# Spreading per-token factors over partitions: a trip through DRAM in place of transposes and selector products

## The chip, the cores and the metric

One core of a Trainium2 chip runs the whole program once. The metric is the device time of that execution in microseconds (us). TensorE multiplies matrices into PSUM, VectorE, ScalarE and GpSimd do the elementwise work, and transfers are issued from the queues of SyncE (SP), ScalarE and GpSimd. In the profile's rows PE is TensorE's matmuls, PEld its weight loads, DVE is VectorE, ACT ScalarE, POOL GpSimd; a name with a q behind it is that engine's own instruction queue.

## The reference, cut to what matters

The layer is a decoder block on 512 tokens of 1024 channels in float32. It has three mixers (gated delta rule, convolution, attention to a memory), merged through gates, and then a gated MLP. The change touches the gated delta rule alone, and there the keys k, four heads of 128 channels:

```
kb = k * beta[..., None]
A = jnp.where(strict, jnp.einsum('bnhid,bnhjd->bnhij', kb, k) * decay, 0.0)
T = lax.linalg.triangular_solve(eye + A, ...)      # inverse of eye + A
u = T @ (v * beta);  w = T @ (kb * exp(g));  then a scan over the chunks
```

Here k is L2-normed per token and head, so the factor of one token and head is beta over the norm of k. The kernel keeps k transposed (channels on partitions, tokens along the row), so a factor per token has to lie along the row, and the same row has to be on all 128 partitions.

## The kernel before, in words

**Tiling.** Activations are held as 128 channels x 512 tokens (S = 512). Every float32 operand of a projection is split into a rounded part and the rest (`split`, L147 to L154: a cast by ScalarE at L150, a subtraction by VectorE at L151), and each 128x128 tile of weights gives three matmuls (L271 to L273). I call those three matmuls a step; eight steps make one output tile of 128 channels, and eight weight tiles make one transfer of 512 KB, a chunk (`fetch`, L232; the transfer is L243).

**Order of the work.** The instructions of TensorE and of the SP queue run in the order of the source. Those of the other engines are ordered by the framework's planner, which simulates the program; a dependency without a semaphore (`paced`, L276, and `behind`, L107) tells only the planner that one instruction comes after another. The source order is made of generators: `run(main, (g, n))` (L158) takes one step of the projection `main`, then lets the background generator g go on by one turn for every n steps. `pause(n)` uses up n turns. The dictionary WAIT (L21) holds the pauses.

**The loops around the change.** The projections of k, q, v and z take 32 steps each (L943 to L951), then comes the first branch loop of 96 steps (L983). In the background run, one behind the other: `l2` (norms of k, transposed copies), `gdn_k` (L688), `base_load`, `gdn_q`, `base_inverse`, `invert` (L780), `scan` and `out`.

- `gdn_k` makes three factors per token and head on VectorE (L690 to L692), tokens on partitions, 128x16. The factor kbc is turned into rows by `rows` (L305): two VectorE instructions split it, four TensorE transposes put it on 8 partitions (L313), ScalarE copies it to krow (L314). A product with a selector column then spreads one head's row over 128 partitions (L703), and VectorE multiplies k with it from PSUM (L705). The products k times kb follow (L715), four blocks of eight 128x128 products, and VectorE multiplies in the decay (L716). Each block goes to DRAM (d_in, L717).
- `base_load` reads the diagonal 32x32 blocks back (L746), `base_inverse` inverts them on VectorE, 62 instructions in one dependent chain (L759, L762, in the rows also L118), stores the result to DRAM (L768, L769) and loads it back as tc32 (L772), all on the SP queue.
- `invert` puts the inverses of larger blocks together. It copies the blocks of tc32 into tm and tts (L794 on ScalarE, L797 on GpSimd, L799 on ScalarE), makes 64 products of 32x32 (L804), copies them out of PSUM to m1 (L807), and after six turns uses m1 in 128 products of 32x32 (L813, L814). Two more levels follow (L829, L838).

The weights are fetched three to four chunks ahead of the step that uses them, on the same SP queue.

Of the kernel before, what the change touches and what calls it, by code (L numbers as in the profile page):

```python
# [9 lines left out]
F32 = mybir.dt.float32  # L10
F32R = mybir.dt.float32r
AF = mybir.ActivationFunctionType
ALU = mybir.AluOpType
AX = mybir.AxisListType

P = 128
S = 512
# [1 line left out]
LAG = (5, 6, 2)  # L19

WAIT = {"mem": 4, "x": 30, "decay": 15, "scores": 1, "level": 6, "scan": 3, "out": 8,  # L21
        "k": 20, "head": 7, "krow": 6, "inverse": 16, "store": 5, "load": 14, "z": 4, "kk": 1, "ln": 30, "mix": 0}
WARM = 10

EARLY = 8
# [7 lines left out]
H = 4  # L33
NT = S // P
# [25 lines left out]
def hybrid_kernel(ctx: ExitStack, tc: tile.TileContext, xT, memT, xtok, mtok, wall, wdn, nfin, vecs, cms, y):  # L60
    nc = tc.nc
# [6 lines left out]
    dp = ctx.enter_context(tc.tile_pool(name="dp", bufs=1, space=bass.MemoryType.DRAM))  # L68
# [7 lines left out]
    def nm(p):  # L76
        uid[0] += 1
        return f"{p}{uid[0]}"
# [5 lines left out]
    def T(shape=(P, S), dt=F32, n="t"):  # L84
        i = slots.popleft()
        t = tp.tile(list(shape), dt, name=nm(n), tag=f"slot{i}")
        owner[t.tensor.name] = i
        return t

    def free(*ts):  # L90
        for t in ts:
            slots.append(owner.pop(t.tensor.name))

    def C(shape, dt=F32, n="c"):
        return cp.tile(list(shape), dt, name=nm(n))
# [4 lines left out]
    def G(shape=(P, S)):  # L100
        return psg.tile(list(shape), F32, name=nm("g"), tag="g")

    def SM(shape):
        return pss.tile(list(shape), F32, name=nm("sm"), tag="sm")

    A, G_, PE = nc.scalar, nc.gpsimd, nc.tensor
# [17 lines left out]
    V = _Vector()  # L124
# [5 lines left out]
    def f(t):  # L130
        return t.bitcast(F32)

    def sl(t):
        return slice(t * P, (t + 1) * P)
# [50 lines left out]
    def pause(n):  # L185
        for _ in range(n):
            yield
# [25 lines left out]
    ps = G()  # L213
# [62 lines left out]
    def paced(ins):  # L276

        tc.add_manual_dep(ins.ins, last[0].ins.name,
                          mybir.DependencyInfo(mybir.DependencyClass.NoSync, mybir.DependencyReason.DATA),
                          reason="pace")  # L280
# [24 lines left out]
    def rows(src, nt, nq, rt):  # L305

        hl = C((P, nt, 2 * nq), F32R)
        V.tensor_copy(hl[:, :, :nq], src)
        V.tensor_tensor(hl[:, :, nq:], src, f(hl[:, :, :nq]), op=ALU.subtract)
        yield from pause(1)  # L310
        ps = SM((P, S))
        for t in range(nt):
            PE.transpose(ps[:2 * nq, sl(t)], f(hl[:, t]), ident)  # L313
        A.copy(rt, ps[:2 * nq, :nt * P])  # L314
        yield

    def squares(tiles, add, pool=()):
# [118 lines left out]
    def C16():  # L436
        return C((P, NT, H))
# [5 lines left out]
    sel4 = const.tile([8, 4], F32R, name="sel4")  # L443
# [14 lines left out]
    def decay():  # L458
# [34 lines left out]
        V.tensor_copy(mg, ps[:, 3])  # L493
        yield from pause(3)
        yield from rows(mg, NT, H, grow)
        yield from pause(2)
        for h in range(H):
# [155 lines left out]
    q, k_, v = [], [], []  # L653
    qe, rk = C16(), C16()
    kbc, kgc, kdc = C16(), C16(), C16()
    at = [T((P, H, P), n="at") for _ in range(NT)]
# [6 lines left out]
    def cb(c16, t):  # L663
        return c16[:, t].unsqueeze(2).to_broadcast([P, H, P])
# [23 lines left out]
    def gdn_k():  # L688
        yield from pause(2)
        V.tensor_tensor(kbc, beta, rk, op=ALU.mult)  # L690
        V.scalar_tensor_tensor(kgc, kbc, -1.0, eg, op0=ALU.mult, op1=ALU.mult)
        V.tensor_tensor(kdc, ekd, rk, op=ALU.mult)  # L692
        yield from pause(WAIT["krow"])
        krow = T((8, S), F32R, n="krow")
        for h in range(H):
            kt = ktok[h][:, :NT - 1]
            G_.tensor_tensor(kt, kt, kdc[:, :NT - 1, h].unsqueeze(2).to_broadcast([P, NT - 1, P]), op=ALU.mult)
        yield from rows(kbc, NT, H, krow)
        yield from pause(2)
        kb = []  # L700
        for h in range(H):
            ps = G()
            PE.matmul(ps, sel4[:, h:h + 1].to_broadcast([8, P]), krow, start=True, stop=True)  # L703
            t = T(n="kb")
            V.tensor_tensor(t, k_[h], ps, op=ALU.mult)  # L705
            kb.append(t)
            yield
        free(krow)
        yield from pause(WAIT["kk"])
        wr = d_in.rearrange("(t b) x -> t (b x)", t=NT * H)[:, :P * P].rearrange("t (p i) -> p t i", p=P)  # L710
        for t in range(NT):
            G_.tensor_tensor(dec[t], dec[t], cb(rk, t), op=ALU.mult)
            ps = G((P, H, P))
            for h in range(H):
                PE.matmul(ps[:, h], k_[h][:, sl(t)], kb[h][:, sl(t)], start=True, stop=True)  # L715
            V.tensor_tensor(at[t], ps, dec[t], op=ALU.mult)  # L716
            A.dma_start(wr[:, t * H:(t + 1) * H], at[t])  # L717
            yield
        free(*kb)

    def gdn_q():
        yield from l2(qe, q, None)
# [57 lines left out]
    def invert():  # L780


        lo = [slice(64 * p, 64 * p + 32) for p in range(2)]
        up = [slice(64 * p + 32, 64 * p + 64) for p in range(2)]
        tc_ = tc32.rearrange("p (t h) a c -> p t h a c", t=NT)
        tm = [T((P, 2, H, 64), n="tm") for _ in range(2)]
        for t in range(NT):
            tts[t] = T((P, H, P), n="tt")
        for m in (*tm, *tts):
            G_.memset(m, 0.0)  # L790
        for b in range(NB):
            r = slice(32 * b, 32 * b + 32)
            for i in range(2):
                A.copy(tm[i][r, :, :, 32 * (b % 2):32 * (b % 2) + 32], tc_[r, 2 * i:2 * i + 2, :, 0])  # L794
            for t in range(NT):
                if t < 2:
                    G_.tensor_copy(tts[t][r, :, r], tc_[r, t, :, 1])  # L797
                else:
                    A.copy(tts[t][r, :, r], tc_[r, t, :, 1])  # L799
        ps = G((P, NT, H, 32))  # L800
        for t in range(NT):
            for h in range(H):
                for a, b in zip(lo, up):
                    PE.matmul(ps[b, t, h], at[t][a, h, b], tc_[a, t, h, 0], start=True, stop=True)  # L804
        m1 = T((P, NT, H, 32), n="m1")
        for b in up:
            A.copy(m1[b], ps[b])  # L807
        yield from pause(WAIT["level"])
        px, py = G((P, NT, H, 32)), G((P, NT, H, 32))
        for t in range(NT):  # L810
            for h in range(H):
                for a, b in zip(lo, up):
                    PE.matmul(px[b, t, h], tc_[b, t, h, 1], m1[b, t, h], start=True, stop=True)  # L813
                    PE.matmul(py[a, t, h], m1[b, t, h], tc_[b, t, h, 1], start=True, stop=True)  # L814
        for i in range(2):
            for b in up:
                V.tensor_scalar(tm[i][b, :, :, :32], px[b, 2 * i:2 * i + 2], -1.0, None, op0=ALU.mult)
        for t in range(NT):
            for a, b in zip(lo, up):
                A.activation(tts[t][a, :, b], py[a, t], AF.Copy, scale=-1.0)  # L820
        free(m1)
        yield from pause(WAIT["level"])
        a, b = slice(0, 64), slice(64, P)
        m1 = []
        for i in range(2):
            ps = G((P, 2, H, 64))
            for t in range(2):
                for h in range(H):
                    PE.matmul(ps[b, t, h], at[2 * i + t][a, h, b], tm[i][a, t, h], start=True, stop=True)  # L829
            m1.append(T((P, 2, H, 64), n="m1"))  # L830
            A.copy(m1[i][b], ps[b])
        free(*at, *tm)
        yield from pause(WAIT["level"])
        for i in range(2):
            ps = G((P, 2, H, 64))
            for t in range(2):
                for h in range(H):
                    PE.matmul(ps[a, t, h], m1[i][b, t, h], tts[2 * i + t][b, h, b], start=True, stop=True)  # L838
            for t in range(2):
                V.tensor_scalar(tts[2 * i + t][a, :, b], ps[a, t], -1.0, None, op0=ALU.mult)  # L840
        free(*m1)
        yield from pause(WAIT["level"])
# [70 lines left out]
    def out(t):  # L913
# [19 lines left out]
        if t == NT - 1:  # L933
            for z in sz:
# [8 lines left out]
    run(proj_conv(k_, 4), (gl, 1), (gd, 1), (gm, 2), (gc, 2))  # L943
    drain(gd)
    gk = chain(gl, gdn_k())
    run(proj_conv(q, 0), (gk, 1.3), (gm, 2), (gc, 3))
    drain(gm)
# [3 lines left out]
    run(proj_z(), (gp, 2))  # L951
    behind[0] = None
    gi = chain(gp, pause(WAIT["load"]), invert(), scan(0),
               rr(scan(1), out(0)), rr(scan(2), out(1)), rr(scan(3), out(2)), out(3))

# [75 lines left out]
    for o in range(KD):  # L1031
        a, b = T(dt=F32R, n="mgh"), T(dt=F32R, n="mgl")
# [359 lines left out]
```

## Time and profile before

| what | value |
|---|---|
| median of 3 runs | 848.01 us (847.92 to 849.87) |
| the profiled execution | 850.48 us, of which the traced span is 848.7 us |
| mean granted TensorE clock | 0.995 |
| TensorE matmul busy | 837.2 us, 99% of the span |
| VectorE, ScalarE, GpSimd busy | 71%, 46%, 10% |
| transfers | 123.22 MB, mean 145 GB/s |

A matmul's busy time is modelled and matmuls overlap, so how fast TensorE goes is read from the starts of its matmuls and not from its busy share. A row of the timeline has the start, the duration, the engine, the source line, the operation, what it writes and reads, its size and count, and in brackets the idle time before it with what ended it. A granted clock of 1.00 is 2.4 GHz, 0.50 is 1.2 GHz.

### The profile page before, as it was taken

How to read it: one execution, taken by the hardware profiler on the slowest of the kernel's cores; microseconds unless marked ns; L12 is line 12 of the kernel's file. 1: busy time of each engine (PE TensorE's matmuls, PEld its weight loads, DVE VectorE, ACT ScalarE, POOL GpSimd, SP SyncE). 2: the span in 40 equal slices, each digit the busy share in tenths (PEclk: the TensorE clock that was granted, in tenths of full speed). 3: DMA queues.
4: the chain of work that ended last, by engine and by line, in shares of the span. 5: the costliest groups of instructions: out<-in, count | busy, mean ns of one | idle time of the engine just before them, and what ended most of it. 6: DMA issues, size and time to landing. Idle time of an engine off the chain costs nothing.

```text
span 848.7 us, 11144 instructions
## 1 busy us (share of the span) xinstructions
PE 837.2 (99%) x4140; PEld 695.1 (82%) x4140; DVE 606.3 (71%) x954; ACT 388.0 (46%) x669; POOL 87.6 (10%) x101
## 2 busy tenths in 40 slices
PE   9999999999999999999999999999999999999996
PEld 7888788788887888888888888888888888888885
DVE  5885799859988999683266556666666656769863
ACT  7854675534235345452334344333333333657443
POOL 0100002500020001032000031111120110000001
PEclk9999999999999999999999999999999999999998
DMA  9753212242063122322244469696896882275662
GB/s 320 294 183 125 75 51 75 78 121 100 25 166 108 51 75 75 100 74 100 100 149 149 149 163 234 182 209 169 211 222 161 229 206 99 76 222 174 223 186 99
DMA packets 60949, 123.22 MB, mean 145 GB/s; under 512 B 18048, under 2 KB 20352, under 8 KB 60544
## 3 DMA queue, kind: packets, MB, share of 16 engines
q1 hardware_dynamic: 47424, 107.84, 38.0%
q0 software_dynamic: 6336, 11.54, 9.0%
q10 hardware_dynamic: 7136, 3.15, 1.3%
q8 instruction: 32, 0.52, 0.3%
q14 instruction: 21, 0.17, 0.1%
HBM read 118.83 MB, written 26.74 MB: 172 GB/s over the span
## 4 chain that ended last, share of the span: by engine, by line
PE 94%; DVE 4%; issue 1%; ACT 1%; POOL 0%; POOLq 0%; DVEq 0%; ACTq 0%
PE mm L271 19%; PE mm L272 18%; PE mm L273 18%; PE g L272 5%; PE g L273 5%; PE g L271 5%; PE g L1261 2%; PE g L1262 2%; PE g L1263 2%; PE mm L1262 2%; PE mm L1261 2%; PE mm L1263 2%; DVE wlo L151 1%; PE g L570 1%; PE g L572 1%
## 5 line engine op out<-in xcount | busy, mean ns | idle before, releaser
L150 ACT CAST whi<-raw 128x1024 fp32r<-128x1024 f32 (+1 forms) x167 | 171.6, 1028 | 277.1 <-PE mm L272 167.9
L151 DVE TENSOR_TENSOR wlo<-raw,whi 128x1024 fp32r<-128x1024 f32 (+1 forms) x167 | 201.3, 1205 | 77.5 <-ACT whi L150 76.6
L271 PE MATMUL mm<-hh,whi 128*128 128x512 f32 x352 | 142.6, 405 | 0.0
L273 PE MATMUL mm<-hh,wlo 128*128 128x512 f32 x352 | 137.6, 391 | 0.0
L272 PE MATMUL mm<-hl,whi 128*128 128x512 f32 x352 | 137.4, 390 | 0.0
L608 DVE SCALAR_TENSOR_TENSOR cc<-u,vec,cc 128x507 f32<-128x507 f32 (+19 forms) x120 | 86.7, 732 | 1.0
L273 PEld LDWEIGHTS mm<-hh,wlo 128*128 128x128 f32 x352 | 66.1, 188 | 14.3
L271 PEld LDWEIGHTS mm<-hh,whi 128*128 128x128 f32 x352 | 66.3, 188 | 13.1 <-issue 1.5
L272 PEld LDWEIGHTS mm<-hl,whi 128*128 128x128 f32 x352 | 66.4, 189 | 11.5
L271 PE MATMUL g<-fh,whi 128*128 128x512 f32 x176 | 69.1, 392 | 0.0
L271 PE MATMUL mm<-fh,whi 128*128 128x512 f32 x176 | 68.9, 392 | 0.0
L273 PE MATMUL mm<-fh,wlo 128*128 128x512 f32 x176 | 68.6, 390 | 0.0
L273 PE MATMUL g<-fh,wlo 128*128 128x512 f32 x176 | 68.6, 390 | 0.0
L272 PE MATMUL g<-fl,whi 128*128 128x512 f32 x176 | 68.6, 390 | 0.0
L272 PE MATMUL mm<-fl,whi 128*128 128x512 f32 x176 | 68.6, 390 | 0.0
L1096 POOL DMA_DIRECT2D q<-wdn x44 | 36.3, 1000 | 160.1 <-DMA q<-q 97.2
L1163 DVE TENSOR_TENSOR fg<-mm,rfb 128x512 f32<-128x512 f32 x22 | 15.2, 691 | 52.1 <-PE mm L273 52.1
L273 PEld LDWEIGHTS mm<-fh,wlo 128*128 128x128 f32 x176 | 33.1, 188 | 6.9
L273 PEld LDWEIGHTS g<-fh,wlo 128*128 128x128 f32 x176 | 33.0, 188 | 6.9
L272 PEld LDWEIGHTS mm<-fl,whi 128*128 128x128 f32 x176 | 33.1, 188 | 6.7
L271 PEld LDWEIGHTS mm<-fh,whi 128*128 128x128 f32 x176 | 33.0, 188 | 6.8
L271 PEld LDWEIGHTS g<-fh,whi 128*128 128x128 f32 x176 | 33.1, 188 | 6.7
(311 smaller groups left out, 1586.4 us busy)
## 6 DMA issues: line engine op xcount, KB each, us to landing
raw<-wall SPq DMA_DIRECT2D x120, 512.0 KB, 3.4
q<-wdn POOLq DMA_DIRECT2D x44, 256.0 KB, 6.4
raw<-q SPq DMA_DIRECT2D x44, 256.0 KB, 2.9
raw<-wdn SPq DMA_DIRECT2D x33, 256.0 KB, 3.4
q<-wdn SPq DMA_DIRECT2D x22, 256.0 KB, 4.5
q<-q SPq DMA_DIRECT2D x22, 256.0 KB, 4.9
x<-xT SPq DMA_DIRECT2D x16, 256.0 KB, 3.9
raw<-wall SPq DMA_DIRECT2D x8, 256.0 KB, 5.5
```

The costliest lines, as they stand in the source:

```text
L150: A.copy(hi, src)
L151: eng.tensor_tensor(lo, src, f(hi), op=ALU.subtract)
L271: PE.matmul(ps, hi, xh[k], start=(k == 0), stop=False)
L272: PE.matmul(ps, hi, xl[k], start=False, stop=False)
L273: last[0] = PE.matmul(ps, lo, xh[k], start=False, stop=(k == n - 1))
L570: PE.matmul(ps[h], hi, xh[k], start=(k == 0), stop=False)
L608: paced(V.scalar_tensor_tensor(a[:, s:], u[c][:, :S - s], vc("dww", c * 31 + 30 - s), a[:, s:], op0=ALU.mult, op1=ALU.add))
L1096: paced(G_.dma_start(dst[p - 3], b[p - 3], accum_op=ALU.add))
L1163: V.tensor_tensor(g, ps, rfb, op=ALU.mult)
L1261: PE.matmul(ps[m], h[:, o:o + P], hi, start=(p == 0), stop=False)
L1262: PE.matmul(ps[m], h[:, o:o + P], lo, start=False, stop=False)
L1263: last[0] = PE.matmul(ps[m], l[:, o:o + P], hi, start=False, stop=(p == NP - 1))
```

## The change

`rows` and the selector product stay for another factor (in `decay`); in `gdn_k` they are replaced. A new helper writes kbc to DRAM, turned round, by one transfer from SP, and after a pause reads each head's row back to all 128 partitions, by four transfers from SP. VectorE multiplies k with these rows in place. Pauses are changed: krow 6 to 3, the new krows 6, kk 1 to 6 and one more behind it, inverse 16 to 18. The four factor multiplications on GpSimd (L697) come three turns sooner. In `invert`, the block copies are put behind the 64 products and the copies to m1 in the source.

```diff
     def spread(dst, src, n, lag):
+        d = dp.tile([NT * n, P], F32, name=nm("rows"))
+        nc.sync.dma_start(d.rearrange("q p -> p q"), src.rearrange("p t h -> p (t h)"))
+        d = d.rearrange("(t h) p -> h t p", h=n)
+        yield from pause(lag)
+        for h in range(n):
+            dst.append(T((P, NT, P), n="row"))
+            nc.sync.dma_start(dst[h], d[h].unsqueeze(0).to_broadcast([P, NT, P]))
+        yield
...
-        krow = T((8, S), F32R, n="krow")
...
-        yield from rows(kbc, NT, H, krow)
-        yield from pause(2)
-        kb = []
+        row, kb = [], []
+        yield from spread(row, kbc, H, WAIT["krows"])
+        yield from pause(WAIT["kk"])
         for h in range(H):
-            ps = G()
-            PE.matmul(ps, sel4[:, h:h + 1].to_broadcast([8, P]), krow, start=True, stop=True)
-            t = T(n="kb")
-            V.tensor_tensor(t, k_[h], ps, op=ALU.mult)
+            t = row[h].rearrange("p t c -> p (t c)")
+            paced(V.tensor_tensor(t, k_[h], t, op=ALU.mult))
             kb.append(t)
-            yield
-        free(krow)
-        yield from pause(WAIT["kk"])
+            if h % 2:
+                yield
+        yield from pause(1)
...
         for m in (*tm, *tts):
             G_.memset(m, 0.0)
+        ps = G((P, NT, H, 32))
+        for t in range(NT):
+            for h in range(H):
+                for a, b in zip(lo, up):
+                    PE.matmul(ps[b, t, h], at[t][a, h, b], tc_[a, t, h, 0], start=True, stop=True)
+        m1 = T((P, NT, H, 32), n="m1")
+        for b in up:
+            A.copy(m1[b], ps[b])
         for b in range(NB):
...
-        ps = G((P, NT, H, 32))
-        for t in range(NT):
-            for h in range(H):
-                for a, b in zip(lo, up):
-                    PE.matmul(ps[b, t, h], at[t][a, h, b], tc_[a, t, h, 0], start=True, stop=True)
-        m1 = T((P, NT, H, 32), n="m1")
-        for b in up:
-            A.copy(m1[b], ps[b])
         yield from pause(WAIT["level"])
```

## Rows read from the trace of the kernel before

**Rows 1.** The page: busy time by engine, and the chain that ended last.
```profile
PE 837.2 (99%) x4140; PEld 695.1 (82%) x4140; DVE 606.3 (71%) x954; ACT 388.0 (46%) x669; POOL 87.6 (10%) x101
...
PE 94%; DVE 4%; issue 1%; ACT 1%; POOL 0%; POOLq 0%; DVEq 0%; ACTq 0%
```

**Rows 2.** Timeline of TensorE around the transposes L313 (start, duration, work).
```profile
162.74 0.39 PE L273 MATMUL mm<-hh,wlo 128*128 128x512 f32 x1
164.04 0.60 PE L313 MATMUL sm<-cm,c 128*8 128x128 f32 x4 [0.92 <-DVE c L309]
164.40 0.48 PE L271 MATMUL mm<-hh,whi 128*128 128x512 f32 x1
```

**Rows 3.** Timeline of TensorE from the first selector product L703 to L715.
```profile
167.01 0.39 PE L273 MATMUL mm<-hh,wlo 128*128 128x512 f32 x1
167.33 0.49 PE L703 MATMUL g<-krow,sel 8*128 8x512 f32 x1
...
168.09 0.39 PE L272 MATMUL mm<-hl,whi 128*128 128x512 f32 x1
...
171.28 0.49 PE L703 MATMUL g<-krow,sel 8*128 8x512 f32 x1
...
173.20 1.05 PE L715 MATMUL g<-kb,qkv 128*128 128x128 f32 x8
```

**Rows 4.** Timeline of TensorE around the products L813 and L814.
```profile
256.67 0.39 PE L272 MATMUL mm<-hl,whi 128*128 128x512 f32 x1
256.90 0.39 PE L273 MATMUL mm<-hh,wlo 128*128 128x512 f32 x1
258.15 0.21 PE L813 MATMUL g<-m,c 32*32 32x32 f32 x1 [0.86 <-ACT m L807]
...
259.93 0.56 PE L271 MATMUL mm<-och,whi 128*128 128x512 f32 x1
...
263.68 0.39 PE L271 MATMUL mm<-och,whi 128*128 128x512 f32 x1
```

**Rows 5.** Timeline of ScalarE from the first block copy to m1.
```profile
251.00 0.71 ACT L794 COPY tm<-c 32x256 f32<-32x256 f32 x2 [1.68 <-DMA c<-d_out]
...
257.52 1.18 ACT L807 COPY m<-g 32x512 f32<-32x512 f32 x2
```

**Rows 6.** Busy time by window: length, engines with counts, PEclk, DMA share, GB/s.
```profile
252.00:254.00 2.00, 2.00 (x25) 1.64 (x19) 2.00 (x4) 1.98 (x8) 1.92 (x5) 1.00 1.04 420
...
261.00:262.00 1.00, 1.00 (x4) 0.71 (x3) 1.00 (x2) 0.96 (x4) 0.00 (x0) 0.50 0.76 250
```

**Rows 7.** Timeline of TensorE at the 64 products L804.
```profile
251.06 1.20 PE L804 MATMUL g<-c,at 32*32 32x32 f32 x64
252.19 0.50 PE L271 MATMUL mm<-hh,whi 128*128 128x512 f32 x1
```

**Rows 8.** Timeline of VectorE: the factor kbc, and the last multiplication of k.
```profile
158.96 1.01 DVE L690 TENSOR_TENSOR c<-c,c 128x16 f32<-128x16 f32 x1
...
171.81 0.69 DVE L705 TENSOR_TENSOR kb<-qkv,g 128x512 f32<-128x512 f32 x1
```

**Rows 9.** DMA issues: what, queue, count, KB each, median us to landing.
```profile
raw<-wall SPq DMA_DIRECT2D x120, 512.0 KB, 3.4
...
d_in<-at ACTq DMA_DIRECT2D x4, 256.0 KB, 2.7
...
c<-d_out SPq DMA_DIRECT2D x1, 512.0 KB, 5.1
...
d_out<-ti SPq DMA_DIRECT2D x2, 128.0 KB, 3.7
...
vec<-vecs SPq DMA_DIRECT2D x1, 8.0 KB, 1.8
```

**Rows 10.** Timeline of the SP queue: the inverses stored, and tc32 loaded.
```profile
238.60 0.61 SPq L768 DMA_DIRECT2D d_out<-ti  x1
...
245.81 0.39 SPq L772 DMA_DIRECT2D c<-d_out  x1
```

More of the change, by code (lines that the diff above doesn't have):

```diff
@@ L21 @@
 WAIT = {"mem": 4, "x": 30, "decay": 15, "scores": 1, "level": 6, "scan": 3, "out": 8,
-        "k": 20, "head": 7, "krow": 6, "inverse": 16, "store": 5, "load": 14, "z": 4, "kk": 1, "ln": 30, "mix": 0}
+        "k": 20, "head": 7, "krow": 3, "krows": 6, "inverse": 18, "store": 5, "load": 14, "z": 4, "kk": 6, "ln": 30, "mix": 0}
 WARM = 10
@@ L314, in rows, with spread @@
         A.copy(rt, ps[:2 * nq, :nt * P])
+        yield
+    def spread(dst, src, n, lag):
+        d = dp.tile([NT * n, P], F32, name=nm("rows"))
[5 more added lines that the diff above has]
+            nc.sync.dma_start(dst[h], d[h].unsqueeze(0).to_broadcast([P, NT, P]))
         yield
@@ L718, in gdn_k @@
             yield
-        free(*kb)
+        free(*row)
     def gdn_q():
```

## The prediction

> **What bounds the kernel now.** I began with the page: TensorE is busy for 99% of the span, and the chain that ended last is 94% TensorE [rows 1]. So only two things shorten the time: matmuls that disappear from TensorE's queue, and times at which that queue stands still or runs slowly. Then I asked which instructions TensorE waits for, and went to the timeline of each place that the diff touches, reading starts of matmuls. In a projection a matmul starts 0.23 us after the last one (256.67 to 256.90) [rows 4], so a step of three is 0.68 us. Anything above that pitch between two projection matmuls is what the inserted work cost. Three such places belong to the change: the four transposes with a wait for VectorE's split of the factor [rows 2], the four selector products [rows 3], and the products L813 and L814, which wait for ScalarE's copy of m1 [rows 4]. At the last one the reader is to see a second loss behind the first: the projection matmuls that follow run slowly until 263.68, at a granted clock of 0.50, the lower level of 1.2 GHz, after TensorE had stood idle and done small products [rows 4, 6].
>
> **The change, part by part.** The sum is made on the profiled execution: 850.48 us, 1.78 above its span. The median of the runs is 848.01, 2.47 lower, and the difference is taken off that median.
>
> *Transposes removed.* From the matmul before them to the one behind them pass 164.40 - 162.74 = 1.66 us; without them 0.23. Gain **1.4 us**, 0.9 of it the wait [rows 2]. VectorE's two splits and ScalarE's copy go too; both lie beside TensorE, so I count nothing.
>
> *Selector products removed.* From the projection matmul ahead of one to the second behind it pass 168.09 - 167.01 = 1.08 us in place of 2 x 0.23. That is 0.62 for each, more than the 0.49 that the product lasts, because the queue also pauses before and after it. There are four: gain **2.5 us** [rows 3].
>
> *Copies of m1 ahead of the block copies.* ScalarE starts its sixteen block copies at 251.00, and m1 only at 257.52 [rows 5], though the 64 products were done at 252.19 [rows 7]. TensorE reaches L813 right behind 256.90 and is through at 259.93: 2.8 us beyond the pitch [rows 4]. With m1 first, its two copies (1.18 us together) end near 254 and nothing waits. What do the 128 products then need? At the pace of L804 (64 in 251.06 to 252.19, 1.13) 2.3 us, with a lead of 0.1 about 2.4: gain 0.4. If the whole block runs as it did after the first start, 258.15 to 259.93 less the second, shorter wait, it needs some 1.3: gain 1.5. Neither row is plainly the nearer (one is the same shape on other data, the other was backed up by the wait), so I take the middle, **0.9 us**. The block copies move some 3 us later; their next user on TensorE is the level behind this one, six turns on, or 4 us.
>
> *The slow stretch.* From 259.93 to 263.68 nine matmuls took 3.75 us instead of 2.07 [rows 4]. If the idle time ahead of them goes, I expect the clock to hold, since behind the L804 block, of products as small but without such a wait, the granted clock was 1.00 [rows 6, 7]. Gain **1.7 us**, or none.
>
> *The trip through DRAM.* kbc is done at 158.96 + 1.01 = 160.0 [rows 8]; the write is queued on SP before that and waits there. It has 128 x 16 = 2048 pieces of 4 bytes. The store of the inverses has 64 x 32 = 2048 pieces of 64 bytes and lands in 3.7 us; a plain 8 KB load lands in 1.8 [rows 9]. I take 3.7, as it has the same number of pieces: 163.9. Then four reads of 256 KB in pieces of 512 bytes, as the stores of d_in have, which land in 2.7; SP needs about 0.6 to issue each [rows 9, 10], so the last lands near 168.6. At the rate of the weight loads (512 KB in 3.4) 1 MB would take 6.8: 170.9. When does TensorE want the result? L715 stood behind step 6 of the v projection at 173.20 [rows 3]. Counting turns, it now stands behind step 10: four steps later (+2.7) with 4.0 us taken out ahead of it (the first two gains): 171.9. The VectorE products are planned in pairs behind steps 7 and 8, so the last pair begins near 170.5 and takes 2 x 0.69 [rows 8]; with one convolution instruction of about that length among them it ends at 172.6. A wait of 0 to 0.7 us; with a write twice as slow and reads of 6.8, 174.6 plus 0.7 for the last product, a wait of 3.4. I take **0.6 us** lost.
>
> *What queues behind the write.* SP waits for kbc, and the weight load behind it (three chunks ahead of its user, 24 steps or 16 us) is issued after 160.3 and lands 3.4 later [rows 9]. The next one stands behind the reads and goes at about 166. TensorE wants the first 24 steps into the v projection, near 181. So nothing is lost, as long as the trip stays under some 15 us.
>
> *Later users.* L804 moves from step 40 to step 47 of the branch loop (+4.8 us, less the 4.0): TensorE is there at about 251.8, plus 0.6. It needs tc32, which was issued at 245.81 and landed 5.1 later, at 250.9 [rows 9, 10], just ahead of L804. VectorE's chain that feeds it should begin and end within 1 us of before, as L715 is hardly moved in time, and a weight load that stood between the store and the load of tc32 now falls ahead of both. I take no wait. GpSimd's multiplications come sooner; their users are the scans. `scan` and `out` move six to seven steps later; TensorE shows no wait there now, and I count nothing.
>
> Sum: 1.4 + 2.5 + 0.9 + 1.7 - 0.6 = 5.9 us. 848.01 - 5.9 = **842.1 us** (844.6 for a profiled execution like the one shown).
>
> **Rivals.**
> *Half of it.* ScalarE's order is the planner's, not the source's; it may leave m1 behind other work, or the clock may fall behind 128 small products in any case. Then the last two gains go: 1.4 + 2.5 - 0.6 = 3.3, **844.7 us**. For it: weight casts and gate activations compete for ScalarE there. Against: in source order m1 now comes first, and it is ready first.
> *The wait moves to L804.* TensorE is 4 us ahead of before, and VectorE's convolution work is paced to TensorE, so it crowds the inversion chain sooner. If the chain ends up to 4 us late, tc32 lands at 254.9 against 252.4: 2.5 us of waiting, and another slow stretch of 1.7. 6.5 - 0.6 - 2.5 - 1.7 = 1.7: **846.3 us**. For it: tc32 landed less than 0.2 us ahead of L804 [rows 7, 9, 10]. Against: L804 was put 0.8 us later in time and one load less stands ahead of tc32.
> *The rows come late, and it is slower.* Place: the wait of VectorE's products for the rows, and L715 behind it, with everything on TensorE's queue held up. Price: each us that the rows land later than about 171 is a us of TensorE. A wait of 3.4 with a slow stretch gives 6.5 - 3.4 - 1.7 = 1.4, 846.6. It turns into a loss over 0.3% (2.5 us) once the wait is over 9 us, or 7.3 with the slow stretch: rows landing behind 178.5, a trip of 18.5 us where I reckon with 8.6 to 11. A write of four times the row's 3.7 us does that: with 14.8 the write lands at 175.0, the rows 4.7 behind it, the last product is done at 180.4, a wait of 8.5: 6.5 - 8.5 - 1.7 = -3.7, **851.7 us**. For it: no transfer in this trace has pieces of 4 bytes. Against: 2048 pieces of 64 bytes took 3.7 us, and the same count of pieces of 256 bytes (tc32) 5.1, so it is bytes that added time there, not pieces [rows 9].
> The Trainium skill, "DMA: Bandwidth & Descriptors", Rules for kernel authors, speaks against this write: it says that a plain DMA with a rearranged access pattern in place of a hardware transpose is 19 times slower, and that a last dimension which isn't contiguous costs one descriptor per element. By that rule, as an estimate, 19 x 1.8 = 34 us for the write, TensorE would wait about 28 us and the time would be near 871 us; no run here shows it yet, and the 3.7 us row speaks against such a factor.
>
> **How the numbers follow.** Forecast 0.56; half of it 0.17; wait at L804 0.11; rows somewhat late, between 845.5 and 850.5, 0.09; slower by the rows 0.07 (0.02 of it the factor of 19). The forecast's own span is 840.9 (m1 gains 1.5, no wait at L715) to 844. The range goes from 840.5 to 846.5: it takes in the forecast and the next two rivals, 0.84, and leaves out the late rows. About 0.3%, 2.5 us, is what a measurement here can tell from no change: below 845.5 lie the forecast, the half and a little of the third (0.75), above 850.5 the late rows (0.07), the rest between (0.18).
>
> **What would show it.** In the changed trace no L313 at the keys and no selector product there, and the first L715 near 172.5. The transfer of the factors to DRAM should land in 2 to 5 us, the rows by 171, and L715 should show a wait below 1 us. At L813 there should be no wait for m1, and the clock should stay at 1.00 from 255 to 265. L804 should show no wait for tc32. The prediction is wrong if L715 waits for more than 3 us, if the slow stretch turns up again at any of these blocks, or if ScalarE still copies m1 last.

## The result, and the profile after

The changed kernel takes **853.97 us** (median of four runs, 853.70 to 854.39) against 847.96 before: a ratio of 1.0068, interval 1.0056 to 1.0081. It is slower by 6.0 us; the forecast was 842.1, 5.9 faster, and the range ended at 846.5. The rival with the late rows, at 0.07, is what came.

The first view is the wait list of TensorE in the changed kernel (what waited, for what, us in total, times, longest).

```profile
PE g L724 <- DVE row L714: 6.5, 2, 6.0
PE g L215 <- DVE warm L211: 1.5, 1, 1.5
```

L724 is what L715 was: the products k times kb. The waits for the split of the factor and for m1 are gone, and one wait of six microseconds has come. Where it starts is in the timeline of the SP queue and the list of DMA issues of the changed kernel (columns as in [rows 9, 10]).

```profile
159.95 0.38 SPq L321 DMA_DIRECT2D rows<-c  x1
160.42 0.80 SPq L243 DMA_DIRECT2D raw<-wall  x1
172.82 2.03 SPq L326 DMA_DIRECT2D row<-rows  x4
174.94 18.26 SPq L243 DMA_DIRECT2D raw<-wall  x6
```

```profile
row<-rows SPq DMA_DIRECT2D x4, 256.0 KB, 4.8
rows<-c SPq DMA_DIRECT2D x1, 8.0 KB, 12.8
```

The write of the factors, L321, goes out at 159.95, where the prediction had it (160.0), and lands **12.8 us** later; 3.7 was forecast. The four reads, L326, leave at 172.8 and not at 163.9. They too are slower than I had them, 4.8 us in the median against 2.7. The chain of waits puts 12.81 us on the write, and lets the last read end at 179.97.

What that does to TensorE is in its timeline (start, duration, work), which answers to [rows 3].

```profile
171.52 0.39 PE L273 MATMUL mm<-hh,wlo 128*128 128x512 f32 x1
177.96 2.34 PE L724 MATMUL g<-row,qkv 128*128 128x128 f32 x6 [6.05 <-DVE row L714]
180.74 0.79 PE L724 MATMUL g<-row,qkv 128*128 128x128 f32 x2 [0.45 <-DVE row L714]
181.19 0.77 PE L271 MATMUL mm<-hh,whi 128*128 128x512 f32 x1
...
182.61 1.91 PE L724 MATMUL g<-row,qkv 128*128 128x128 f32 x8
184.18 0.77 PE L271 MATMUL mm<-hh,whi 128*128 128x512 f32 x1
...
185.30 1.05 PE L724 MATMUL g<-row,qkv 128*128 128x128 f32 x8
186.11 0.48 PE L271 MATMUL mm<-hh,whi 128*128 128x512 f32 x1
...
186.89 1.05 PE L724 MATMUL g<-row,qkv 128*128 128x128 f32 x8
```

In the kernel before the same place looks like this:

```profile
172.97 0.39 PE L273 MATMUL mm<-hh,wlo 128*128 128x512 f32 x1
173.20 1.05 PE L715 MATMUL g<-kb,qkv 128*128 128x128 f32 x8
174.00 0.48 PE L271 MATMUL mm<-hh,whi 128*128 128x512 f32 x1
```

TensorE reaches the place at 171.52 + 0.23, as forecast (171.9). From 171.52 to 181.19 pass 9.67 us; without a wait 1.03 (in the kernel before 172.97 to 174.00). That is 8.6 lost. The next two rounds, from one L271 to the next, take 2.99 and 1.93 us against 1.59 between the last two blocks: 1.4 and 0.3 more, for the clock had fallen. The windows show it (length, busy time of PE, PEld, DVE, ACT, POOL with counts, then the granted clock, DMA share, GB/s): full up to 174, then the lower level of 1.2 GHz for nearly all of the next ten. Before it fell, TensorE had started nothing since the matmul at 171.52.

```profile
170.00:174.00 4.00, 1.91 (x9) 1.25 (x7) 0.00 (x0) 0.00 (x0) 0.00 (x0) 1.00 0.42 75
174.00:184.00 10.00, 5.57 (x18) 4.47 (x19) 6.06 (x8) 3.78 (x5) 0.00 (x0) 0.53 0.85 297
```

Loss at this place: 8.6 + 1.4 + 0.3 = **10.4 us**. Against it stand the gains. Ahead of it TensorE is at 171.52 where the kernel before would be at 172.97 + 4 x 0.68 = 175.7: 4.2 us (3.9 forecast). And the 128 products no longer wait; here is TensorE around them in the changed kernel, which answers to [rows 4].

```profile
267.11 0.39 PE L273 MATMUL mm<-hh,wlo 128*128 128x512 f32 x1
...
268.65 0.50 PE L271 MATMUL mm<-hh,whi 128*128 128x512 f32 x1
268.99 0.39 PE L272 MATMUL mm<-hl,whi 128*128 128x512 f32 x1
```

From the matmul ahead to the one behind pass 1.54 us in place of 3.03: 1.5 gained, the upper end of what I had given it. The sum, 10.4 - 4.2 - 1.5 = 4.7, is 1.3 short of the 6.0 measured. The traces bear the 4.7 out: from the first projection matmul to the last the changed kernel takes 710.6 us (28.88 to 739.47), and e2, a kernel below that is as fast as before and has no slow stretch in its trace, 705.8 (28.42 to 734.19), which is 4.8 less. Of the rest, 0.5 lies ahead of the first projection matmul of these two; what remains is no more than executions of one kernel differ by, and I do not place it. In the profiled executions of before and of the changed kernel the spans differ by only 3.2, because the one shown of before had a slow stretch of 1.7 that its median does not have. Of 33 further executions of before, four took 849.9 to 850.0 us at a mean granted clock of 0.995, as the profiled one has, and the other 29 took 847.7 to 848.8 us at 0.997 to 0.999.

### The profile page after: what moved, and what is told of

It reads as the page before. It is cut to its first block, busy times and chain, and to the rows that moved or that the text cites. A ratio compares the mean times of both kernels' runs of the same rounds, so it can differ in the third digit from the quotient of the medians.

```text
span 851.9 us, 11143 instructions
## 1 busy us (share of the span) xinstructions
PE 835.9 (98%) x4132; PEld 695.5 (82%) x4132; DVE 604.7 (71%) x952; ACT 387.6 (46%) x668; POOL 87.8 (10%) x101
## 4 chain that ended last, share of the span: by engine, by line
PE 92%; DVE 3%; DMA 2%; issue 1%; ACT 1%; POOL 0%; SPq 0%; POOLq 0%; DVEq 0%; ACTq 0%
PE mm L271 18%; PE mm L273 18%; PE mm L272 18%; PE g L271 5%; PE g L273 5%; PE g L272 5%; PE g L1272 2%; PE g L1271 2%; PE g L1270 2%; PE mm L1272 2%; PE mm L1271 2%; PE mm L1270 2%; DMA rows<-c 2%; PE g L582 1%; PE g L583 1%; PE g L584 1%
## 5 line engine op out<-in xcount | busy, mean ns | idle before, releaser
L271 PE MATMUL mm<-hh,whi 128*128 128x512 f32 x352 | 142.5, 405 | 0.0
L620 DVE SCALAR_TENSOR_TENSOR cc<-u,vec,cc 128x503 f32<-128x503 f32 (+21 forms) x120 | 86.6, 733 | 0.9
L271 PEld LDWEIGHTS mm<-hh,whi 128*128 128x128 f32 x352 | 66.5, 189 | 12.3 <-issue 0.5
L271 PE MATMUL g<-fh,whi 128*128 128x512 f32 x176 | 69.0, 392 | 0.0
L271 PE MATMUL mm<-fh,whi 128*128 128x512 f32 x176 | 68.9, 391 | 0.0
L272 PEld LDWEIGHTS g<-fl,whi 128*128 128x128 f32 x176 | 33.1, 188 | 6.7
L271 PEld LDWEIGHTS g<-fh,whi 128*128 128x128 f32 x176 | 33.1, 188 | 6.6
```

The lines of the kernel that those rows point to most:

```text
L271: PE.matmul(ps, hi, xh[k], start=(k == 0), stop=False)
L272: PE.matmul(ps, hi, xl[k], start=False, stop=False)
L620: paced(V.scalar_tensor_tensor(a[:, s:], u[c][:, :S - s], vc("dww", c * 31 + 30 - s), a[:, s:], op0=ALU.mult, op1=ALU.add))
```

## The experiments

The theory: the write of 4-byte pieces is slow by itself, and TensorE waits for what depends on it. Against it stood that the reads and SP's queue hold the rows up whatever the write does, and that the weight load stuck behind the write does the damage.

**e3, the same rows by a cheap write.** Only the write is changed: the 128x16 factor is turned by one TensorE transpose and stored in 16 pieces of 512 bytes. The four reads stay.

```diff
-        nc.sync.dma_start(d.rearrange("q p -> p q"), src.rearrange("p t h -> p (t h)"))
+        ps = SM((NT * n, P))
+        PE.transpose(ps, src.rearrange("p t h -> p (t h)"), ident)
+        turned = C((NT * n, P))
+        A.copy(turned, ps)
+        nc.sync.dma_start(d, turned)
```

> The changed kernel with the factors turned round on TensorE (one transpose of 128x16 into PSUM, one copy by ScalarE) and stored as 16 pieces of 512 bytes; the four reads stay. Theory A: the write lands within 2 to 3 us in place of 12.8, the reads are issued near 164 and land by 171, the wait at the first k times kb product falls from 6 us to under 1.5, and the clock stays at 1.00: 842 to 845 us. Rival B (the reads, 7 us in the changed kernel, and SP's queue hold the rows up whatever the write does): the rows land behind 174, a wait of 2 to 5 us with a slow stretch stays, 846 to 850 us.

Measured: **843.00 us** (842.87 to 843.28), ratio 0.9932 to before, 0.9915 to 0.9948. It is the best version of the study (with e7, which differs from it only in `invert`), 11 us under the changed kernel. First its DMA issues, then TensorE at the products (L728 here).

```profile
row<-rows SPq DMA_DIRECT2D x4, 256.0 KB, 5.8
rows<-c SPq DMA_DIRECT2D x1, 8.0 KB, 1.4
```

```profile
171.20 0.39 PE L273 MATMUL mm<-hh,wlo 128*128 128x512 f32 x1
171.43 1.05 PE L728 MATMUL g<-row,qkv 128*128 128x128 f32 x8
```

The same 8 KB land in 1.4 us, and TensorE goes from the projection to the product without a gap. The reads are no faster than in the changed kernel (5.8 us in the median), so they are not the cause: they are early enough. A transpose on TensorE cost a tenth of a microsecond there: the matmuls on both sides of it, 158.84 and 159.09, are 0.25 apart, and the next step comes 0.1 late.

**e8, the write on ScalarE's queue.** Now the weight load no longer stands behind the write on SP.

```diff
-        nc.sync.dma_start(d.rearrange("q p -> p q"), src.rearrange("p t h -> p (t h)"))
+        A.dma_start(d.rearrange("q p -> p q"), src.rearrange("p t h -> p (t h)"))
```

> The changed kernel with the write of the factors issued from ScalarE's queue in place of SP's. Theory A (the 4-byte pieces themselves are slow on the transfer engines): the write lands in 11 to 13 us again, the rows come as late, 853 to 855 us, though the weight load that stood behind it on SP's queue lands in 4 to 8 us and ScalarE and VectorE no longer stand still for it. Rival E (the weight load behind the write, 14 us late, is what held VectorE's products): the products no longer wait, 846 to 850 us.

Measured: 853.11 us, ratio 1.0060 (1.0043 to 1.0077). The issue and VectorE's first product in e8:

```profile
rows<-c ACTq DMA_DIRECT2D x1, 8.0 KB, 12.3
```

```profile
175.49 0.69 DVE L714 TENSOR_TENSOR row<-qkv,row 128x512 f32<-128x512 f32 x1 [9.23 <-DMA row<-rows]
```

The write is as slow on the other queue, and VectorE's first product now waits for nothing but the rows. No other transfer is under way meanwhile, and the windows of e8 show what the slow write looks like (columns as above):

```profile
159.50:164.00 4.50, 4.50 (x22) 3.72 (x21) 4.34 (x8) 1.33 (x3) 4.50 (x4) 1.00 0.21 2
164.00:172.00 8.00, 7.52 (x34) 5.89 (x32) 1.31 (x1) 2.01 (x3) 3.74 (x4) 1.00 0.00 0
```

The 8 KB move before 164 (2 GB/s in 4.5 us). Then the transfer engines show nothing, 0.00, until the write counts as landed near 171.9 and the reads leave. So the 12.3 us are not spent behind other transfers, and for the most part not in engines that work on the pieces, as theory A had it. What the time behind 164 goes to, the trace does not show. In the changed kernel the picture is less clear, since ScalarE waits there for the load behind the write (13.5 us, until 174.87) with VectorE's split behind it; e8 shows that this wait is not what costs.

**e9, the products later.** If only the arrival counts, pauses should do as well.

```diff
-        "k": 20, "head": 7, "krow": 3, "krows": 6, "inverse": 18, "store": 5, "load": 14, "z": 4, "kk": 6, "ln": 30, "mix": 0}
+        "k": 20, "head": 7, "krow": 3, "krows": 6, "inverse": 18, "store": 5, "load": 6, "z": 4, "kk": 15, "ln": 30, "mix": 0}
```

> The changed kernel with the pause before the products raised from 6 to 15 turns and the pause before the inversion's use cut from 14 to 6, so that k times kb stands nine steps (6.1 us) later on TensorE's queue and what follows about where it was. Theory A: only the time at which the rows arrive counts; the wait of 8.6 us at the first product falls to some 2.5, too short for a slow stretch: gain 6 + 1.7, 845 to 848 us. Rival F (the wait moves to tc32 or to the branch that uses the result, since the whole chain behind is as late as before): 849 to 853 us.

Measured: 860.73 us, ratio 1.0151 (1.0135 to 1.0166), worse than either theory had it. TensorE's waits in e9:

```profile
PE g L884 <- ACT vn L877: 4.0, 1, 4.0
PE mm L271 <- DVE qkv L649: 3.8, 1, 3.8
PE g L724 <- issue: 2.9, 1, 2.9
```

The wait splits up and grows. First the projection itself stands still, for L649, which empties its PSUM: VectorE, in e9, stands idle for 11.2 us ahead of the split that comes before L649, until 175.04, because that split waits for ScalarE's cast and the cast for the weight load behind the write.

```profile
175.04 1.23 DVE L151 TENSOR_TENSOR wlo<-raw,whi 128x1024 fp32r<-128x1024 f32 x1 [11.21 <-ACT whi L150]
176.18 2.31 DVE L649 SCALAR_TENSOR_TENSOR qkv<-mm,vec,qkv 128x511 f32<-128x511 f32 x3
```

So the load behind the write does no harm only as long as TensorE stands still anyway; with the products out of the way it is the next bound. Then L724 still waits 2.9: its products on VectorE stand behind one more split (183.42), which waits 4.9 for the cast of the next weight load. These two waits, 6.7 together, are as much as the 6.5 of the changed kernel. What comes on top is the 4.0 at the scan and a clock of 0.73 and 0.85 in the eight microseconds from 294. There TensorE waits for ScalarE's copy of vn:

```profile
295.02 0.59 ACT L877 COPY vn<-g 128x512 f32<-128x512 f32 x1 [6.76 <-DVE cc L118]
```

The products that it copies were done near 289.6; the trace names VectorE's convolution as what it waited for last, and no run shows why that comes so late in e9. My expectation had only the rows in mind.

**e1 and e2, each half alone.** e1 is the changed kernel with the 64 products and the copies to m1 put back behind the block copies; e2 is the kernel before with that reordering alone. The edit is the block of the diff above, backwards and forwards.

> The changed kernel with the products L804 and the copies to m1 put back behind the block copies; the trip through DRAM and all pauses stay. Theory A (the 2048 pieces of 4 bytes make the write slow, and TensorE waits for its rows): the same 9 to 10 us between the neighbouring projection matmuls at the first k times kb product, write landing 12 to 13 us, 853.5 to 855.5 us. If the reordering is worth the 3.2 us that the two profiles show at this place, it is lost again only if m1 is late once more; TensorE reaches the 64 products 5 us behind tc32 in the changed kernel, when the block copies are done, so I expect no wait at m1 and no difference: 854.0 +- 0.8.

> The kernel before with nothing but the reordering: the 64 products and the copies to m1 ahead of the block copies. If the wait for m1 and the slow stretch behind it are in every run of before, 845 to 846.5 us (0.9 to 1.5 and 1.7 less). Rival: the runs without them make up before's median already (the profiled execution of before is 2.5 us above it), and the reordering is worth the wait alone or nothing: 846.5 to 848. In the trace: m1 copied within 2 us of the 64 products, 1.3 us for the 128 products, granted clock 1.00 behind them.

Measured: e1 852.76 us (1.0052, 1.0032 to 1.0073), e2 848.26 us (0.9998, 0.9989 to 1.0007). All of the loss is in the trip through DRAM, and the reordering alone does nothing. Both medians miss what I had expected, e1 by 0.7 us below its range (its runs spread from 852.17 to 855.38), e2 by 0.3 above its rival's. ScalarE's timeline in e2 says why (L802 are block copies, L798 the copies to m1):

```profile
250.30 0.71 ACT L802 COPY tm<-c 32x256 f32<-32x256 f32 x2 [1.38 <-DMA c<-d_out]
...
256.83 1.18 ACT L798 COPY m<-g 32x512 f32<-32x512 f32 x2
```

With L798 ahead of L802 in the source, the planner still puts it last, behind sixteen block copies and two casts. The change does not do there what its diff says. TensorE's wait for m1 is as long as in before, and yet the clock is full behind it (a line of the wait list, and a window that answers to the second of [rows 6]):

```profile
PE g L813 <- ACT m L798: 1.2, 2, 0.8
```

```profile
261.00:262.00 1.00, 1.00 (x6) 0.83 (x5) 1.00 (x3) 0.87 (x4) 0.00 (x0) 1.00 0.90 328
```

**e7**, e3 with the reordering taken back, agrees:

> The kernel of the turned store (e3) with the 64 products and the copies to m1 put back behind the block copies. In e3 the planner left the copies to m1 behind the block copies all the same, and TensorE did not wait since L804 stands later against tc32. If so, putting them back changes nothing: 842.6 to 843.4. If the source order had a part in it, 844 to 845.

Measured: 843.24 us (0.9941, 0.9926 to 0.9956), no different from e3. Why then has the wait for m1 gone in the changed kernel and in e3? Because L804 comes some five microseconds behind tc32 there and the block copies are over when it is through. That the order in the source has no part in it is shown by e1 and e7: they have the old order, and neither has a wait for m1. **e11** tries that on the kernel before, by one number:

```diff
-        "k": 20, "head": 7, "krow": 6, "inverse": 16, "store": 5, "load": 14, "z": 4, "kk": 1, "ln": 30, "mix": 0}
+        "k": 20, "head": 7, "krow": 6, "inverse": 16, "store": 5, "load": 20, "z": 4, "kk": 1, "ln": 30, "mix": 0}
```

> The kernel before with nothing but the pause ahead of the inversion's use raised from 14 to 20 turns, so that the 64 products L804 stand some six steps (4.5 us) later and the block copies are done when they come, as in the changed kernel. If the gain at L813 comes from the place of L804 against tc32 and not from the order in the source: no wait for m1, the block of 128 products needs 1.3 us in place of 2.8, 846.3 to 847.0 us. Rival: something behind it is late in turn (the branch that uses the result), 848 us or more.

Measured: 847.70 us, ratio 0.9989 (0.9980 to 0.9999). TensorE around the products in e11:

```profile
260.82 0.39 PE L273 MATMUL mm<-hh,wlo 128*128 128x512 f32 x1
261.83 0.21 PE L813 MATMUL g<-m,c 32*32 32x32 f32 x1 [0.35 <-ACT m L807]
...
263.01 0.50 PE L271 MATMUL mm<-hh,whi 128*128 128x512 f32 x1
```

2.19 us in place of 3.03, where the changed kernel has 1.54: a little over half of the loss is gone by timing alone. It is not all, since tc32 landed later too: ScalarE's first block copy starts at 252.55 and not at 251.00, and L804 at 255.71 stands only 3.2 us behind it, against 5.3 in the changed kernel. The direction holds; the gain of half a microsecond is less than the 1.2 to 2 I expected.

**e5 and e10, the price of a write.** Both add four writes of a 128x16 factor, or of a part of it, to the kernel before, in the branch loops, each waiting for a VectorE copy made there so that the queue ahead is empty. Their own times (864.96 and 864.34 us) tell nothing, since those waits hold the weight loads up. The core of e5 and of e10 (the remarks behind # are mine):

```diff
+        nc.sync.dma_start(d1.rearrange("q p -> p q"), late())                   # turned
+        nc.sync.dma_start(d2[:n // 2].rearrange("q p -> p q"), late()[:, :n // 2])
+        nc.sync.dma_start(d3[:, :, 0], late())                                  # apart: d3 is 128 x 16 x 16
+        nc.sync.dma_start(d4, late())                                           # plain: d4 is 128 x 16
...
+        nc.sync.dma_start(d1.rearrange("q p -> p q"), late()[:P // 2])          # half: 64 partitions
+        nc.sync.dma_start(d2.rearrange("q p -> p q"), late()[:, :n // 4])       # four rows
+        nc.sync.dma_start(d3.rearrange("q p x -> p q x")[:, :, 0], late())      # loose: d3 is 16 x 128 x 16
+        nc.sync.dma_start(d4.rearrange("q p x -> p q x")[:, :, 0], late())      # pair: d4 is 16 x 128 x 2
```

> The kernel before with four writes of a 128x16 factor to DRAM tiles that nobody reads, in the second and third branch loops, 49 steps (33 us) apart, each waiting for a VectorE copy made at that step, so that no weight load and no other probe is under way ahead of it. In order: turned, 2048 pieces of 4 bytes; turned, 1024 pieces; 2048 pieces of 4 bytes, each 64 bytes from the next; plain, 128 pieces of 64 bytes. Theory A (a price per piece of 4 bytes): 12.8, about 7, 11 to 13, about 2 us. Rival C (it is the neighbouring 4-byte pieces of different partitions in one stretch of DRAM that hinder each other): 12.8, about 7, 3 to 6, about 2 us.

> Four more writes in the kernel before, at the same places and with the same waits as in e5. There half as many turned pieces (8 rows of 128) took 11.9 us and 16 rows of 128 took 12.7, so it is not their number; pieces set 64 bytes apart took 6.6. Theory G (the pieces of one row of 512 bytes go in one after another, about 84 ns each, the rows beside each other): 16 rows of 64 pieces (half the partitions) about 7 us; 4 rows of 128 about 12; 16 rows of 128 with the pieces 64 bytes apart about 6.6; with the pieces 8 bytes apart about 12 or, if a stretch shorter than the row counts, 7 to 9. Rival H (the turned order itself is slow, adjacent or not): 64 bytes apart in the turned order takes 12 us as well.

The issues of e5, then of e10 (last column us to landing):

```profile
turned<-c SPq DMA_DIRECT2D x1, 8.0 KB, 12.7
turned<-c SPq DMA_DIRECT2D x1, 4.0 KB, 11.9
apart<-c SPq DMA_DIRECT2D x1, 8.0 KB, 6.6
plain<-c SPq DMA_DIRECT2D x1, 8.0 KB, 2.2
```

```profile
half<-c SPq DMA_DIRECT2D x1, 4.0 KB, 10.7
four<-c SPq DMA_DIRECT2D x1, 2.0 KB, 10.1
loose<-c SPq DMA_DIRECT2D x1, 8.0 KB, 5.6
pair<-c SPq DMA_DIRECT2D x1, 8.0 KB, 8.9
```

Each figure is of one execution; the turned write of 2048 pieces occurs in six of them and took 12.3 to 13.0 us. Weight loads follow half a microsecond behind each probe, but the plain write took 2.2 us with them, and in e8 the turned one took 12.3 without.

It is not the number of pieces: 2048 take 12.7 us, 1024 take 11.9 or 10.7, 512 still 10.1. It is not the turned order either: in the same order, with each piece 64 bytes from the next, 2048 pieces take 5.6. What counts most is how close the pieces lie: 4 bytes apart 12.7, 8 bytes 8.9, 64 bytes 5.6. A price per piece (theory A, and my 84 ns of theory G) is refuted, by the half that took 10.7 and not 7. Why close pieces hinder each other, no run here shows.

**e4, a probe that told little.** An earlier form of e5 with the four writes eight steps apart in the v projection.

> The kernel before with four more writes of a 128x16 factor to DRAM tiles that nobody reads, eight steps apart on the SP queue. Theory A (a fixed price per 4-byte piece): the turned write of 2048 pieces lands in 11 to 13 us; the turned write of half as many in 6.5 to 7.5; the write of 2048 pieces of 4 bytes, each to a line of its own 64 bytes apart, in 11 to 13 too; the plain write (16 factors of a token together) in 2 to 2.5. Rival C (neighbouring pieces of 4 bytes that fall into one stretch of DRAM hinder each other): the pieces set apart land in 3 to 5 us, like the 2048 pieces of 64 bytes of the store of the inverses (3.7). Rival D (the price is a share of the queue with the weight load): all four differ by how a weight load stands to them and not by their form.

The first write landed in 12.7 us. The others were issued while an earlier probe or a weight load was still under way (the plain one took 8.0, against 2.2 in e5), so they measure the queue and not their form. That is why e5 sets them further apart (28 to 47 us in its trace).

## Why the prediction was wrong

By its own steps:

- *Transposes and selector products, 1.4 + 2.5.* Right: 4.2 us where the sum had 3.9.
- *The trip through DRAM.* The step that failed, by one term: "I take 3.7, as it has the same number of pieces". The write took 12.8, and the wait at the products, 0.6 in the sum, became a loss of 10.4. I had picked the row by the count of pieces. In DRAM the row's pieces, of 64 bytes each, start 256 bytes apart; ours start 4 bytes apart. The same misreading stands in the rival's "Against" (bytes, not pieces): number and bytes were the two quantities I compared, closeness was not one. I gave a loss by a slow write 0.07 because no row showed one. No row could: there was no such write in the trace. The factor of 19 in the Trainium skill's "DMA: Bandwidth & Descriptors", Rules for kernel authors, is against the hardware transpose, which no run here has. Put against a plain transfer, as my estimate did, it was too large for this shape (12.7 to 2.2 is 5.8), but it pointed the right way.
- *The reads.* 2.7 us each was too low; they took 4.8 in the changed kernel and 5.8 in e3. In e3 that stayed hidden.
- *What queues behind the write.* I counted how long TensorE can go without the next weights (16 us) and found room. I did not ask who else stands in line: the load behind the write holds ScalarE, ScalarE holds VectorE, and VectorE holds the projection's PSUM. e9 shows that as the next bound.
- *m1 ahead of the block copies, 0.9.* The gain came, 1.5 us, and for another reason than I gave: by the place of L804 and not by the order in the source (e1, e2, e7). In the changed kernel ScalarE still copies m1 last, at 264.71, behind the block copies and three casts.
- *The slow stretch, 1.7.* A gain that was not there to have. The profiled execution of before has it, but e2, with the same wait (1.2 us in all) and the same products, shows a clock of 1.00 behind them and takes 848.26, before's median. I subtracted from the median a loss that belonged to the one execution above it. That its time was 2.5 us over the median was in the table, and I used it only as an offset.
- *Price of the loss.* The rival asked for a write of 14.8 us to give 851.7, with a loss of 8.5 for the wait and 1.7 for the slow stretch, 10.2. A write of 12.8 cost as much, 10.4, because the reads were slower too: the last row landed 7.2 us behind the write, not 4.7. That the time is 854 and not 851.7 lies elsewhere: the rival still counted on 6.5 of gains, and there were 5.7 (4.2 + 1.5): the 1.7 of the slow stretch was missing, and the two others gave 0.9 more. The rest is the 1.3 that the sum above leaves open.

All three signs that the prediction named for being wrong came: a wait of more than 3 us, a slow stretch behind it, and m1 copied last.

With a write of 1.4 us in its place, the gains as measured give 4.2 + 1.5 less 0.1 for the new transpose, 5.6 us; e3 gains 5.2 against its runs of before. The mechanism of the gain was right, and one size turned it round. That the forecast's 5.9 comes so near is partly luck: the 1.7 that was not there is nearly made up by m1 (1.5 for 0.9), by the transposes and products (4.2 for 3.9) and by the 0.6 that e3 does not wait.

## What to carry to other kernels

A transfer that turns a tile in 4-byte pieces should be priced by a run of that very shape, not by a row with as many pieces or as many bytes; turning on TensorE first cost 0.1 us here and made the write nine times faster (1.4 against 12.8 us). Where a chain through DRAM feeds an in-order queue, follow the load behind it as well, through every engine that waits for it. And before a stall seen in one profiled execution is booked as a gain, hold that execution's time against the median.

## What was not expected of the hardware

Three things. Writes of 4-byte pieces into DRAM got cheaper when the same pieces lay further apart: 12.7, 8.9 and 5.6 us at 4, 8 and 64 bytes, for the same 8 KB in the same order, and a quarter of the pieces still took 10.1. The slow write does not look busy: in e8 the transfer engines show no work for the last eight of its twelve microseconds. And the clock behind a short wait is not the same in every execution: after a pair of waits for m1 of nearly the same length (1.2 us in all, in e4 1.1) and the same 128 products it fell to 0.50 in the profiled execution of before [rows 6] and stayed at 1.00 in those of e2 and e4.
